# Tree attention on one core: every GpSimd store behind the last load, and V copies at later steps

## The chip, the cores and the metric

The kernel runs on one core of a Trainium2 chip. The metric is the device time of one execution in microseconds (us). A profiled execution has a span, from its first to its last instruction, and a time of its own that is a little longer than the span.

The core has a matrix engine (TensorE, PE in the profile), VectorE (DVE), ScalarE (ACT), GpSimd (POOL) and SyncE (SP). Transfers between the chip's memory and the core's are issued as instructions of GpSimd, SyncE or ScalarE and are carried out by 16 DMA engines that all of them share.

## The reference

Q, K, V and the output are float32 of shape 8 x 12 x 512 x 64 (batch, heads, positions, width): 96 heads, 12.58 MB each. A position attends to itself and to its ancestors in a binary tree laid over the positions.

```
mask[i, i] = 1
parent = i
while parent > 0:
    parent = (parent - 1) // 2
    mask[i, parent] = 1

scores = einsum('bhqd,bhkd->bhqk', Q, K) * scale
scores = scores + (1 - mask) * (-1e9)
weights = exp(scores - max(scores))
weights = weights / (sum(weights) + 1e-10)
return einsum('bhqk,bhkd->bhqd', weights, V)
```

## The kernel before

The 96 heads are worked on as 48 pairs. The outer loop has one step `i` per pair. In step `i` TensorE makes the scores of pair `i` (`scores1`, `scores2`), ScalarE takes the exponentials, TensorE multiplies the exponentials of pair `i - 1` with V (`values`, tile `ob`), and VectorE normalises pair `i - 1` (`norm`, lines 581 and 583, one reciprocal for a pair) into an output buffer `of` that holds 8 heads. There is one `ob` in the on-chip accumulation memory for all but the last pair, so the values of a pair wait until the pair before is normalised. Then the K (odd steps) or Q (even steps) of two later pairs is transposed by TensorE and copied by VectorE (`turn`: lines 401, 412, 416, 420 for K, 433 and 441 for Q). At the end of the step, VectorE does the V copies that a table gives it for this step.

K and Q come in blocks of 8 heads with four buffers each, V in blocks of 16 heads with three buffers (`vloads`). All these loads are issued by GpSimd, which turns float32 into bfloat16 on the way; V of a block comes in three pieces, "upper", "even" and "odd" rows. From heads 16 on, V is rearranged into tiles `vt` (two sets, used in turn) by copies that `spread` makes, all at line 336:

- "M" and "Y" on VectorE, 8 heads at a time, at the steps that `BY_VECTOR` and `STEADY_VECTOR` name. M needs all three pieces of the load.
- "X", "Z0", "Z1" (`spread_pool`) and four "top" copies (`spread_top`) on GpSimd. X writes over a part of what M wrote, so it comes behind M.

GpSimd works through one list in order, `pool_program`: loads, its own V copies and the stores of the output. A GpSimd instruction that waits holds everything behind it. A load waits until its buffer is free; further, GpSimd's transfers share eight completion counters in turn, so that one is issued only when the eighth before it has landed. `ready` decides only after which step an entry of the list is put into the program.

The list is written out by hand up to heads 56 to 63; from head 64 on a loop makes it. That loop issues K and Q of each block of 8, what is left of V, GpSimd's V copies, and a store of 8 heads as soon as `BEHIND` (56) heads lie between it and the load:

```
while VO * stored + VO + BEHIND <= h + KB:
    ops.append((store, nc.gpsimd, VO * stored, VO))
    stored += 1
```

With the store in the written-out part, four stores of 8 heads (1 MiB each) stand among the loads. The rest of GpSimd's stores stand behind the last load. SyncE stores heads 76 to 79 at step 41 (`store_apart`) and, with ScalarE, the last heads.

`STEADY_VECTOR` puts M of heads 64 to 79 at steps 24 and 26 and Y at 28 and 30; of heads 80 to 95, M at 32 and 34 and Y at 36 and 38.

Of the kernel before, what the change touches and what calls it, by code (L numbers as in the profile page):

```python
# [9 lines left out]

CODE = 2048.0
CODE_ROWS = 40
NOUT = 11
BEHIND = 56

# [104 lines left out]
def kernel(  # L120
# [7 lines left out]
    nc = tc.nc  # L128
# [4 lines left out]
    NH = B * H  # L133
# [3 lines left out]
    KB, VB, VO = 8, 16, 8  # L137
# [28 lines left out]
    small = ctx.enter_context(tc.tile_pool(name="small", bufs=4))  # L166
    opool = ctx.enter_context(tc.tile_pool(name="opool", bufs=NOUT))
    psS = ctx.enter_context(tc.tile_pool(name="psS", bufs=1, space=bass.MemoryType.PSUM))
# [168 lines left out]

    PARTS = ((0, 1, 2, 3, 4, 5, 6, 7, 8, 9), ("M", "X", "Y", "Z0", "Z1", 6, 7, 8, 9))

    def spread_top(o, h0=0, h1=VB):  # L340
        for part in range(6, 10):
            spread(nc.gpsimd.tensor_copy, o, part, h0, h1)

# [263 lines left out]
    def pool_program():  # L607

        ops = [
            (load_k, 2, 2), (load_q, 2, 2), (load_v, 0, 4), (load_v, 4, 4),  # L610
            (load_k, 4, 2), (load_k, 6, 2), (load_q, 4, 2), (load_k, 8, 4),
            (load_q, 6, 2), (load_q, 8, 4), (load_v, 8, 8), (load_k, 12, 4),
            (load_q, 12, 4), (load_k, 16, 4), (load_rows, 1, "upper"),
            (load_q, 16, 4), (load_rows, 1, "even"), (load_k, 20, 4), (load_rows, 1, "odd"),
            (load_q, 20, 4), (load_k, 24, 8), (load_q, 24, 4), (load_rows, 2, "upper"),
            (load_q, 28, 4), (load_k, 32, 4), (load_rows, 2, "even", "odd"),
            (load_q, 32, 8), (load_k, 36, 4), (load_rows, 3, "upper"),
            (spread_pool, (1, "Z0", 8, 16), (1, "Z1", 8, 16)),
            (load_k, 40, 8), (load_q, 40, 8), (load_rows, 3, "even", "odd"),
            (spread_top, 2, 0, 16), (spread_pool, (2, "Z0", 0, 16), (2, "Z1", 0, 16)),  # L620
            (load_q, 48, 4), (spread_pool, (2, "X", 0, 8)),
            (load_k, 48, 8), (spread_pool, (2, "X", 8, 16)),
            (load_q, 52, 4), (load_rows, 4, "upper"), (spread_top, 3, 0, 16),
            (load_k, 56, 8), (load_q, 56, 8), (load_rows, 4, "even", "odd"),
            (spread_pool, (3, "X", 0, 8), (3, "Z0", 0, 16), (3, "Z1", 0, 16), (3, "X", 8, 16)),
            (load_rows, 5, "upper"), (store, nc.gpsimd, 0, VO),
        ]
        loaded, stored = 88, 1
        for h in range(64, NH, KB):
            top = [(spread_top, h // VB + 0)] if h % VB == 8 and 4 <= h // VB + 0 < NH // VB else []  # L630
            ops += [(load_k, h, KB)] + top + [(load_q, h, KB)]
            while loaded < min(h + 32, NH):
                names = ("even", "odd") if loaded % VB else ("upper",)
                ops.append((load_rows, loaded // VB) + names)
                loaded += KB
            if top:
                o = h // VB
                ops.append((spread_pool, (o, "X", 0, 16), (o, "Z0", 0, 16), (o, "Z1", 0, 16)))
            while VO * stored + VO + BEHIND <= h + KB:
                ops.append((store, nc.gpsimd, VO * stored, VO))  # L640
                stored += 1
        for g in range(stored, NH // VO - 1):
            if g == APART // VO:
                ops.append((store, nc.gpsimd, VO * g + 2, APART - VO * g - 2))
            else:
                ops.append((store, nc.gpsimd, VO * g, VO))
        for p0, p1 in zip(SPLIT_ROWS, SPLIT_ROWS[1:]):
            ops.append((store, nc.gpsimd, APART // VO * VO, 2, 1, p0, p1))
        return ops

    def ready(op, i):
# [16 lines left out]
    BY_VECTOR = {  # L668
        0: [(0, 2, 0, 8), (0, 7, 0, 4), (0, 1, 0, 8), (0, 6, 0, 8), (0, 3, 0, 8), (0, 9, 0, 8)],
        1: [(0, 0, 4, 8)],  # L670
        2: [(0, 7, 4, 16), (0, 4, 8, 12)],
        3: [(0, 5, 8, 16), (0, 2, 8, 16), (0, 3, 8, 16)],
        4: [(0, 0, 8, 16)],
        5: [(0, 9, 12, 16)],
        6: [(0, 4, 12, 16)],
        7: [(1, "M", 0, 8), (1, "Y", 0, 8), (1, 7, 0, 8)],
# [9 lines left out]
        20: [(3, "M", 8, 16)],  # L686
        22: [(3, "Y", 0, 8)],
        24: [(3, "Y", 8, 16)],
    }
    BY_SCALAR = {  # L690
# [8 lines left out]
    }  # L699

    STEADY_VECTOR = {0: [("M", 0, 8)], 2: [("M", 8, 16)], 4: [("Y", 0, 8)], 6: [("Y", 8, 16)]}

    def spread_by(copy, table, steady, i):

        o, j = divmod(i, 8)
        todo = table.get(i, [])
        if 4 <= o + 1 < NH // VB:
            todo = todo + [(o + 1,) + piece for piece in steady.get(j, [])]
        for args in todo:
            spread(copy, *args)  # L710

    program = pool_program()
# [23 lines left out]
    for i in range(NP + 1):  # L736
        steps = FIRST[i] if i < len(FIRST) else "SVK" if i % 2 else "SVQ"
        for step in steps:
            if step == "S" and i < NP:
                scores1(i)  # L740
                scores2(i)
            if step == "V" and i >= 1:
                values(i - 1)
                norm(i - 1)
                valued = True
            if step == "K" and kdone < NP:
                kdone = turn("kst", kdone)
            if step == "Q" and qdone < NP:
                qdone = turn("qst", qdone)
            if step == "W":  # L750
                nc.scalar.copy(
                    out=codes[64:64 + CODE_ROWS, 1280:1536], in_=codes[0:CODE_ROWS, 1280:1536]
                )
            if step == "X":
                spin("s1" if valued else "ob", 2)
            if step == "D":
                spread_by(nc.vector.tensor_copy, BY_VECTOR, STEADY_VECTOR, i)
            if step == "A":
                spread_by(nc.scalar.copy, BY_SCALAR, {}, i)
        if "D" not in steps:  # L760
            spread_by(nc.vector.tensor_copy, BY_VECTOR, STEADY_VECTOR, i)
        if "A" not in steps:
            spread_by(nc.scalar.copy, BY_SCALAR, {}, i)
        pool(i)
        if i == APART_AT:
            store_apart()
        if i >= NP - 3 and i < NP:
            store(nc.sync, head(i - 1, 0), 2, 2)
# [33 lines left out]
```

## Time and profile before

| | |
|---|---|
| median of 3 runs | 135.26 us (135.2 to 137.54) |
| the profiled execution's own time | 135.11 us |
| its span | 133.2 us |
| mean granted clock of TensorE | 0.961 |
| busy: PE, DVE, ACT, POOL | 115.8, 100.0, 94.4, 77.2 us |
| read from memory, written to it | 37.94 MB, 12.58 MB |

A row of a timeline gives the start, the duration, the engine and the line, what is written and read, and in brackets how long the engine had been idle before and what ended that. L336 is line 336 of the kernel. Rows with several instructions say xN. A matmul's end is modelled, and a busy PE is not PE at its peak. The rows "DMA to landing" are from an issue to its last byte's completion. In the windows view each row is a stretch of the span, with its length, each engine's busy time, the clock granted to TensorE, the share of the DMA engines and the GB/s that were written.

### The profile page before, as it was taken

How to read it: one execution, taken by the hardware profiler on the slowest of the kernel's cores; microseconds unless marked ns; L12 is line 12 of the kernel's file. 1: busy time of each engine (PE TensorE's matmuls, PEld its weight loads, DVE VectorE, ACT ScalarE, POOL GpSimd, SP SyncE). 2: the span in 40 equal slices, each digit the busy share in tenths (PEclk: the TensorE clock that was granted, in tenths of full speed). 3: DMA queues.
4: the chain of work that ended last, by engine and by line, in shares of the span. 5: the costliest groups of instructions: out<-in, count | busy, mean ns of one | idle time of the engine just before them, and what ended most of it. 6: DMA issues, size and time to landing. Idle time of an engine off the chain costs nothing.

```text
span 133.2 us, 5532 instructions
## 1 busy us (share of the span) xinstructions
PE 115.8 (87%) x2417; PEld 80.3 (60%) x2417; DVE 100.0 (75%) x249; ACT 94.4 (71%) x153; POOL 77.2 (58%) x106
## 2 busy tenths in 40 slices
PE   6987969999898998999979399999898997989920
PEld 2543655766675766677756367677665775666610
DVE  3449779889999999969865666989797897667350
ACT  4369577988889788587858444898866887597900
POOL 6999526354285999968723789525449820005900
PEclk9999999999999999999999757999999999999995
DMA  3999999999999999999999999999999999999993
GB/s 116 233 178 191 199 196 200 202 202 205 199 202 202 202 203 205 200 210 198 206 203 198 317 253 202 292 274 252 319 216 334 231 313 401 400 393 369 379 262 132
DMA packets 32676, 32.27 MB, mean 242 GB/s; under 512 B 1628, under 2 KB 29916, under 8 KB 32652
## 3 DMA queue, kind: packets, MB, share of 16 engines
q0 software_dynamic: 30256, 29.63, 114.5%
q1 hardware_dynamic: 1836, 1.83, 4.2%
q10 hardware_dynamic: 560, 0.46, 1.1%
q8 instruction: 19, 0.31, 0.9%
q14 instruction: 5, 0.04, 0.1%
HBM read 37.94 MB, written 12.58 MB: 379 GB/s over the span
## 4 chain that ended last, share of the span: by engine, by line
PE 41%; DMA 40%; POOL 6%; issue 4%; DVE 3%; ACT 2%; DVEq 0%; ACTq 0%; POOLq 0%
DMA vst<-in_V_dram 40%; PE ob L551 13%; PE s L458 6%; PE s L466 4%; PE qtp L433 4%; PE ktp L401 4%; PE s L501 3%; PE s L491 3%; POOL kst L239 2%; POOL qst L239 2%; DVE of L583 1%; POOL vst L239 1%; PE s L551 1%; DVE vt L336 1%; ACT e L472 1%
## 5 line engine op out<-in xcount | busy, mean ns | idle before, releaser
L476 ACT ACTIVATE e<-s 128x1024 bf16<-128x1024 f32 x40 | 40.9, 1023 | 23.3 <-PE s L466 22.7
L551 PE MATMUL ob<-vt,e 128*128 128x65 bf16 (+1 forms) x940 | 38.3, 199 | 5.0 <-DVE of L583 3.5
L551 PEld LDWEIGHTS <-e 128*128 128x128 bf16 (+1 forms) x960 | 31.0, 104 | 13.4 <-DVE of L583 3.3
L507 ACT ACTIVATE e<-s 128x384 bf16<-128x384 f32 x80 | 34.7, 491 | 0.0
L583 DVE TENSOR_TENSOR of<-ob,rec 128x512 f32<-128x512 f32 x47 | 32.5, 691 | 1.6
L336 POOL COPY vt<-vst 32x512 int32<-32x512 int32 (+1 forms) x32 | 24.1, 753 | 8.8 <-DVE vt L336 4.4
L592 POOL DMA_DIRECT2D out_dram<-of x17 | 14.2, 838 | 15.6 <-DVE of L583 14.5
L336 DVE COPY vt<-vst 64x1024 bf16<-64x1024 bf16 (+6 forms) x42 | 17.9, 427 | 6.0 <-DMA vst<-in_V_dram 5.4
L458 PE MATMUL s<-codes 40*128 40x512 bf16 x96 | 19.9, 402 | 1.3 <-issue 0.7
L581 DVE RECIPROCAL rec<-ob 128x8 f32<-128x8 f32 x47 | 9.6, 205 | 14.4 <-PE ob L551 13.6
L466 PE MATMUL s<-kq 64*128 64x512 bf16 x96 | 18.9, 385 | 0.0
L280 POOL DMA_DIRECT2D vst<-in_V_dram x15 | 10.8, 720 | 13.2 <-DMA vst<-in_V_dram 7.5
L501 PEld LDWEIGHTS <-kq 64*128 64x128 bf16 x320 | 12.7, 95 | 5.5 <-issue 1.2
L501 PE MATMUL s<-kq 64*128 64x160 bf16 (+1 forms) x320 | 15.3, 210 | 0.4 <-issue 0.4
L491 PE MATMUL s<-codes 40*128 40x384 bf16 x80 | 14.1, 339 | 0.3
L401 PE MATMUL ktp<-ptile,kst 128*64 128x128 bf16 x320 | 12.9, 224 | 1.2 <-issue 0.9
L441 DVE COPY kq<-qtp 128x1024 bf16<-128x1024 bf16 x20 | 13.6, 682 | 0.4 <-PE qtp L433 0.3
L433 PE MATMUL qtp<-ptile,qst 128*64 128x128 bf16 x320 | 13.1, 224 | 0.8 <-issue 0.6
L251 POOL DMA_DIRECT2D kst<-in_K_dram x12 | 9.1, 761 | 5.7 <-DMA kst<-in_K_dram 1.5
L251 POOL DMA_DIRECT2D qst<-in_Q_dram x13 | 9.5, 728 | 4.8 <-PE s L501 1.9
L491 PEld LDWEIGHTS <-codes 40*128 40x128 bf16 x80 | 6.3, 96 | 9.3 <-issue 1.3
L472 ACT ACTIVATE e<-s 128x1024 bf16<-128x1024 f32 x8 | 8.2, 1022 | 5.0 <-PE s L466 5.0
(42 smaller groups left out, 121.6 us busy)
## 6 DMA issues: line engine op xcount, KB each, us to landing
out_dram<-of POOLq DMA_DIRECT2D x10, 1024.0 KB, 15.7
kst<-in_K_dram POOLq DMA_DIRECT2D x8, 512.0 KB, 15.2
qst<-in_Q_dram POOLq DMA_DIRECT2D x7, 512.0 KB, 16.2
vst<-in_V_dram POOLq DMA_DIRECT2D x12, 256.0 KB, 14.4
vst<-in_V_dram POOLq DMA_DIRECT2D x6, 512.0 KB, 13.6
qst<-in_Q_dram POOLq DMA_DIRECT2D x8, 256.0 KB, 11.9
kst<-in_K_dram POOLq DMA_DIRECT2D x6, 256.0 KB, 11.8
out_dram<-of SPq DMA_DIRECT2D x4, 256.0 KB, 5.4
```

The source lines that it names most:

```text
L251: return nc.gpsimd.dma_start(out=kept[b][:, h0 % KB:h0 % KB + n, :, :].rearrange("p (g x) t d -> p g (x t d)", x=2), in_=wide[:, h0 // 2:( ...
L336: return copy(out=dst, in_=src)
L401: nc.tensor.transpose(out=columns(kp[64 * a:64 * a + 64, :], mixed, (256, 2), (leaves - mixed, 2), (1, 32)), in_=st[:, 2 * i % KB // 2 + a ...
L433: nc.tensor.transpose(out=halves[64 * a:64 * a + 64, :, c:c + 64], in_=st[:, 2 * i % KB // 2 + a, 4 * u + t, :], identity=ptile[:, 0:128],)
L458: nc.tensor.matmul(out=sp[:, a, :], lhsT=(k1code if i < WIDE else k1wide)[64 * a:64 * a + CODE_ROWS, :], rhs=(q1code[64 * a:64 * a + CODE_ ...
L466: nc.tensor.matmul(out=sp[:, a, :], lhsT=keys(i, a, TOP), rhs=qTs[i][64 * a:64 * a + 64, :, :].rearrange("p t c -> p (t c)"), start=False, ...
L476: ) if i < WIDE else nc.scalar.activation(
L491: nc.tensor.matmul(out=flat[:, a, :, :].rearrange("p u (t c) -> p u t c", t=4)[:, :, :, 16:64], lhsT=k2wide[64 * a:64 * a + CODE_ROWS, :], ...
L501: nc.tensor.matmul(out=flat[:, a, :, lo:hi], lhsT=keys(i, a, WTILE2[t]), rhs=qT[64 * a:64 * a + 64, :, lo:hi], start=False, stop=t == 1, s ...
L507: nc.scalar.activation(out=e2s[i % NE][:, a, :, 32:128].rearrange("p t (r u) -> p t r u", u=2), in_=flat[:, a, :, :].rearrange("p u (t r) ...
L551: nc.tensor.matmul(out=ob[lo:hi, a, 65 * t:65 * t + 65], lhsT=e[:, a, PLACE[t], lo:hi], rhs=vt[vtile[tile_v][0]][:, head(i, a) % VB, vtile ...
L583: nc.vector.tensor_tensor(out=ofs[g][:, first:last + 1:step, :, :], in0=o4[:, a:a + n, :, 0:D], in1=rec[:, a:a + n, :, :].to_broadcast([P, ...
```

## The change

The loop from head 64 on is replaced by a list written out to its end: K and Q of heads 64 to 79, all of V's heads 80 to 95 behind the top copies of heads 64 to 79, then the rest of GpSimd's copies of that block, K and Q of heads 80 to 95, GpSimd's copies of heads 80 to 95, and after these every one of GpSimd's stores. The copies, loads and stores are the same ones as before; the four stores that stood among the loads are now behind them. The output buffers become 12 (each of 8 heads).

`STEADY_VECTOR` goes, and `BY_VECTOR` names the steps for heads 64 to 95 too: M of heads 64 to 79 at 26 and 28 (before 24 and 26), Y at 29 and 30 (before 28 and 30); M of heads 80 to 95 at 36 and 37 (before 32 and 34), Y at 38 and 39 (before 36 and 38).

```
-NOUT = 11
-BEHIND = 56
+NOUT = 12
...
-            (load_rows, 5, "upper"), (store, nc.gpsimd, 0, VO),
+            (load_k, 64, 8), (load_q, 64, 8), (load_k, 72, 8), (spread_top, 4, 0, 16),
+            (load_q, 72, 8), (load_rows, 5, "upper"), (load_rows, 5, "even", "odd"),
+            (spread_pool, (4, "X", 0, 16), (4, "Z0", 0, 16), (4, "Z1", 0, 16)),
+            (load_k, 80, 8), (load_q, 80, 8), (load_k, 88, 8), (load_q, 88, 8),
+            (spread_top, 5, 0, 16),
+            (spread_pool, (5, "X", 0, 16), (5, "Z0", 0, 16), (5, "Z1", 0, 16)),
         ]
-        loaded, stored = 88, 1
-        for h in range(64, NH, KB):
-            top = [(spread_top, h // VB + 0)] if h % VB == 8 and 4 <= h // VB + 0 < NH // VB else []
-            ops += [(load_k, h, KB)] + top + [(load_q, h, KB)]
-            while loaded < min(h + 32, NH):
-                names = ("even", "odd") if loaded % VB else ("upper",)
-                ops.append((load_rows, loaded // VB) + names)
-                loaded += KB
-            if top:
-                o = h // VB
-                ops.append((spread_pool, (o, "X", 0, 16), (o, "Z0", 0, 16), (o, "Z1", 0, 16)))
-            while VO * stored + VO + BEHIND <= h + KB:
-                ops.append((store, nc.gpsimd, VO * stored, VO))
-                stored += 1
-        for g in range(stored, NH // VO - 1):
+        for g in range(NH // VO - 1):
...
+        26: [(4, "M", 0, 8)],
+        28: [(4, "M", 8, 16)],
+        29: [(4, "Y", 0, 8)],
+        30: [(4, "Y", 8, 16)],
+        36: [(5, "M", 0, 8)],
+        37: [(5, "M", 8, 16)],
+        38: [(5, "Y", 0, 8)],
+        39: [(5, "Y", 8, 16)],
     }
...
-    STEADY_VECTOR = {0: [("M", 0, 8)], 2: [("M", 8, 16)], 4: [("Y", 0, 8)], 6: [("Y", 8, 16)]}
```

`spread_by` loses the argument for that table.

More of the change, by code (lines that the diff above doesn't have):

```diff
@@ L338, with spread_top @@
     PARTS = ((0, 1, 2, 3, 4, 5, 6, 7, 8, 9), ("M", "X", "Y", "Z0", "Z1", 6, 7, 8, 9))
-    def spread_top(o, h0=0, h1=VB):
+    def spread_top(o, h0, h1):
         for part in range(6, 10):
@@ L699, with spread_by @@
     }
-    STEADY_VECTOR = {0: [("M", 0, 8)], 2: [("M", 8, 16)], 4: [("Y", 0, 8)], 6: [("Y", 8, 16)]}
[L703 to L709, printed above, removed]
+    def spread_by(copy, table, i):
+        for args in table.get(i, []):
             spread(copy, *args)
@@ L756 @@
             if step == "D":
-                spread_by(nc.vector.tensor_copy, BY_VECTOR, STEADY_VECTOR, i)
+                spread_by(nc.vector.tensor_copy, BY_VECTOR, i)
             if step == "A":
-                spread_by(nc.scalar.copy, BY_SCALAR, {}, i)
+                spread_by(nc.scalar.copy, BY_SCALAR, i)
         if "D" not in steps:
-            spread_by(nc.vector.tensor_copy, BY_VECTOR, STEADY_VECTOR, i)
+            spread_by(nc.vector.tensor_copy, BY_VECTOR, i)
         if "A" not in steps:
-            spread_by(nc.scalar.copy, BY_SCALAR, {}, i)
+            spread_by(nc.scalar.copy, BY_SCALAR, i)
         pool(i)
```

## The prediction

> **What bounds the kernel now.** I read the page's slices first, then the windows view for the rate of the DMA in stretches of one kind, then the timelines of GpSimd and VectorE for the steps that move. The page first:
>
> ```profile
> DMA  3999999999999999999999999999999999999993
> GB/s 116 233 178 191 199 196 200 202 202 205 199 202 202 202 203 205 200 210 198 206 203 198 317 253 202 292 274 252 319 216 334 231 313 401 400 393 369 379 262 132
> HBM read 37.94 MB, written 12.58 MB: 379 GB/s over the span
> ```
>
> The DMA engines are never free between the first slice and the last. The GB/s row counts what is written: a load reads float32 and writes bfloat16, so 200 there is 400 of reading. The windows view gives both kinds (its last two columns are the DMA share and GB/s):
>
> ```profile
> core 0: us, PE busy (x) PEld busy (x) DVE busy (x) ACT busy (x) POOL busy (x), PEclk, DMA share, GB/s
> 6.00:70.00 64.00, 58.62 (x1278) 41.26 (x1274) 54.65 (x135) 50.04 (x80) 42.91 (x59) 1.00 1.35 200
> 112.00:120.00 8.00, 6.73 (x162) 4.80 (x158) 5.37 (x13) 5.92 (x12) 0.00 (x0) 1.00 1.03 398
> ```
>
> From 6 to 70 us only loads run (400 GB/s read), from 112 to 120 us only stores (398 GB/s). One common figure, 400 GB/s or 2.62 us per MiB, turns the 50.5 MB into 126.3 us of pure moving. The last store of the program and its time to landing are these:
>
> ```profile
> L592 ACTq DMA_DIRECT2D out_dram<-of x1: 351/351/351, 128.5 to 128.5; - x1
> DMA to landing us min/median/max: 3.6/3.6/3.6
> ```
>
> It lands at 128.5 + 3.6 = 132.1. So 126.3 of 132.1 us are unavoidable moving, and the rest is the start and the end. That is the first bound: **whatever order the transfers take, a stretch without any is lost**, since nothing later can go faster. The second bound is TensorE, nearly full from 84 us on. It lost time before that. VectorE's timeline (start, duration, engine, line; in brackets the idle time before it and what ended it):
>
> ```profile
> 69.79 0.21 DVE L581 RECIPROCAL rec<-ob 128x8 f32<-128x8 f32 x1 [1.28 <-PE ob L551]
> 71.35 0.42 DVE L336 COPY vt<-vst 64x1024 bf16<-64x1024 bf16 x1
> 74.16 0.43 DVE L336 COPY vt<-vst 128x1024 bf16<-128x1024 bf16 x1 [2.38 <-DMA vst<-in_V_dram]
> 83.17 0.21 DVE L581 RECIPROCAL rec<-ob 128x8 f32<-128x8 f32 x1 [0.86 <-PE ob L551]
> 85.28 0.21 DVE L581 RECIPROCAL rec<-ob 128x8 f32<-128x8 f32 x1
> 87.38 0.21 DVE L581 RECIPROCAL rec<-ob 128x8 f32<-128x8 f32 x1 [0.17 <-PE ob L551]
> 103.45 0.21 DVE L581 RECIPROCAL rec<-ob 128x8 f32<-128x8 f32 x1 [0.50 <-PE ob L551]
> ```
>
> TensorE's timeline behind that, and its clock in the windows view:
>
> ```profile
> 75.48 1.20 PE L551 MATMUL ob<-vt,e 128*128 128x65 bf16 x20 [2.28 <-DVE of L583]
> ```
>
> ```profile
> 66.50:69.80 3.30, 2.60 (x64) 1.83 (x58) 1.90 (x6) 1.88 (x5) 1.06 (x2) 1.00 1.27 203
> 76.00:80.00 4.00, 4.00 (x60) 2.75 (x59) 2.43 (x6) 1.40 (x3) 3.50 (x5) 0.50 1.16 272
> 80.00:84.00 4.00, 4.00 (x80) 2.77 (x82) 2.70 (x7) 2.18 (x5) 3.68 (x4) 0.78 1.32 201
> ```
>
> There is one L581 per pair; counted back from the last pair, 69.79 belongs to pair 23, 83.17 to pair 27 and 103.45 to pair 36. The row at 74.16 is the M copy of heads 64 to 71. VectorE waits 2.38 us in it for V, with pair 24's normalisation queued behind; TensorE has one ob buffer, so it waits 2.28 us for that normalisation, and then works at a granted clock of 0.50 and 0.78 until 84 us. An undisturbed pair takes 87.38 - 85.28 = 2.10 us.
>
> **The V copies later.** M of heads 64 to 71 goes from step 24 to step 26. Its V lands when the DMA chain says:
>
> ```profile
> 58.30 15.67 DMA vst<-in_V_dram
> ```
>
> That is 73.97. At step 26 the copy stands behind pair 25's normalisation: 69.79 + 2 x 2.10 = 73.99, and in step 24 the copy followed its pair's reciprocal by 71.35 - 69.79 = 1.56, so it starts at 75.6, 1.6 us after the landing. I cost the copies themselves at nothing, because they are the same copies. They fit beside the normalisation in a TensorE step; without that cover each costs its 0.42 us. The wait goes, and I take the clock loss with it. Pairs 23 to 27 took 83.17 - 69.79 = 13.38 us and would take 4 x 2.10 = 8.40, so **TensorE is 5.0 us earlier** from pair 27 on. Bounds: all of it, or only the wait of 2.4 us if the clock falls anyway.
>
> On that fall, the Trainium skill, TensorE: Matmul & The Clock Gate, section What's actually happening, says the half rate comes after an idle window of about 3.4 us. The trace disagrees as far as it goes: the gap was 2.28 us, and the clock was at 0.50 right behind it. By the page the gap would be too short to blame, and the fall might come again; the second rival below prices it from the rows.
>
> **The loads in a new order.** Up to the second half of V's heads 64 to 79 (the issue at 58.30) the GpSimd queue is the same. Behind it stood 10 MiB of loads mixed with four stores of 1 MiB, to this last load:
>
> ```profile
> L251 POOL DMA_DIRECT2D qst<-in_Q_dram x1: 740/740/740, 94.0 to 94.0; - x1
> DMA to landing us min/median/max: 16.2/16.2/16.2
> ```
>
> It landed at 110.2: 14 MiB in 36.2 us, 2.59 us each. Without the four stores the loads land at 73.97 + 10 x 2.59 = **99.9 us**, if GpSimd issues in time. The place to check is the load of K from head 80, now behind X, Z0 and Z1 of heads 64 to 79, and X waits for the M copy of step 28: pair 27 at 78.2, the M copy 1.56 later at 79.8, X about 0.6 after it (rows below), three copies in 3.2 us, so K 80 is issued at 83.6. The six MiB issued before it last until 73.97 + 6 x 2.59 = 89.5. The queue does not run dry, with 5.9 us in hand; the rest of the loads follow at about 0.75 us each. K, Q and V all arrive earlier than before, so TensorE gains no new wait.
>
> **The stores behind everything.** Now the first store stands behind X, Z0 and Z1 of heads 80 to 95. X may not run before the second M copy of those heads, and that copy is moved from step 34 to step 37. Step 34 of before (97.79, then GpSimd's two rows) and the K copies of step 37 (104.97) show the price of each piece:
>
> ```profile
> 97.79 0.42 DVE L336 COPY vt<-vst 128x1024 bf16<-128x1024 bf16 x1
> 104.97 0.41 DVE L420 COPY kq<-ktp 128x512 bf16<-128x512 bf16 x1
> ```
>
> ```profile
> 98.34 3.21 POOL L336 COPY vt<-vst 32x1024 int32<-32x1024 int32 x3 [3.60 <-DVE vt L336]
> 101.50 4.57 POOL L592 DMA_DIRECT2D out_dram<-of  x5
> ```
>
> Pair 36 is normalised at 103.45 - 5.0 = 98.5. The K copies of step 37 end 104.97 + 0.41 - 103.45 = 1.93 later, so M starts at 100.4, X follows M's start by 98.34 - 97.79 = 0.55, at 100.9, and the three copies take 101.50 - 98.34 = 3.16. **The first store is issued at 104.1**, where before four stores had gone out between the loads and five more followed from 101.5. In the whole of this stall GpSimd waits for VectorE and nothing else can refill the DMA queue: the last load is long issued, and the stores of SyncE come only with pair 41.
>
> So the DMA engines, which finish their last load at 99.9, have nothing until the first store's data moves. What an issue costs before data moves on empty queues is not shown for GpSimd. The nearest row is a small load at the start:
>
> ```profile
> L184 ACTq DMA_DIRECT2D ptile<-tree_eye x1: 383/383/383, 0.7 to 0.7; - x1
> DMA to landing us min/median/max: 2.6/2.6/2.6
> ```
>
> Its 64 KB take 0.2 us to move, so 2.4 us are fixed. Bounds: from 0.9 (the 4.57 / 5 of one store's issue alone) to 3.6 (the last store's landing, with other stores beside it); I take 2.4, the quietest of the three.
>
> Then all 12.58 MB of output are still to go, 31.4 us at 400 GB/s. Bounds: 31.1 at the 2.59 per MiB of the mixed stretch; 32.9 at what before's last 8 MiB took, 110.2 to 132.1 with its thin end, 2.74 per MiB. Compute is over by 128 - 5 = 123 us, so the small stores of SyncE and ScalarE at the end hide in the backlog, where before they stood open.
>
> The twelfth output buffer costs nothing: 12 buffers of 8 heads hold all 96 heads, so no normalisation waits for a store.
>
> **Sum.** 104.1 + 2.4 + 31.4 = 137.9 us for the last landing. Before, the span of 133.2 ended 1.1 after the last landing, and the profiled execution's own time, 135.11, is 1.9 over its span: 137.9 + 1.1 + 1.9 = **140.9 us**. The median of the runs is 135.26, 0.15 above the profiled one, so I forecast 141.0. In terms of the queue: it is silent for 104.1 + 2.4 - 99.9 = 6.6 us, and 0.8 of that comes back at the end.
>
> The Trainium skill, DMA: Bandwidth & Descriptors, section Anatomy of one DMA, gives about 2.0 us plus the bytes over 436 GB/s for a GpSimd DMA. No run here shows 436; the stretch of stores alone had 398. By the page the last landing would be 104.1 + 2.0 + 28.9 = 135.0 and the time an estimate of 138.0, still over before.
>
> **The rivals.**
>
> *The silent stretch is filled (not slower).* If the stores start before the loads run out, 99.9 + 31.4 = 131.3, and the time is 134.3. The place is the end of the load queue, the point from which it decides is the first issue: up to 99.9 + 0.8 - 2.4 = 98.3 nothing is lost against before. X would have to start at 95.1, 5.8 us sooner than worked out. For it: TensorE's waits on issue and code between pairs 27 and 36 are 20.28 - 9 x 2.10 = 1.4 us, which could shrink. Against: 1.4 is all there is; TensorE is at full clock and busy in that stretch. Chance 0.06.
>
> *The clock falls anyway.* TensorE gets back only the wait. Then pair 36 stands at 103.45 - 2.4 = 101.1, everything behind it moves by 2.6, and the time is 143.6. For it: the clock took until 84 us to recover, so what sets it acts over several us. Against: between 66.50 and 69.80 TensorE stood for 0.7 us (2.60 busy of 3.30) and the clock stayed at 1.00, so only a longer gap is known to lower it, and that gap goes. Chance 0.13.
>
> *Stores alone go faster than 400 GB/s.* For it: no load is beside them for 30 us, and TensorE is done for the last 14. To reach 138.0, the edge of a difference that can be told, the output would have to move in 28.5 us, at 441 GB/s; to be no slower than before in 25.7 us, at 490. Against: the pure stretch of before held 398, with TensorE idle a sixth of it. Chance 0.08.
>
> *The edit does not do what it says*, because GpSimd keeps the queue full only on paper: should X of heads 64 to 79 come over 5.9 us late, the loads run dry too. It can only add. Chance 0.03.
>
> **How the numbers follow.** The forecast has 0.70. From the bounds: 104.1 may be 102.7 (no waits on issue) to 106.7, the start 0.9 to 3.6, the drain 31.1 to 32.9, so 137.7 to 146.2 at the far ends. I cut to 138.0 to 144.5, which takes in the fallen clock and the fast stores. About 2% (2.7 us) is what a measurement of this kernel tells from no change: faster by more than that needs under 132.6, so a filled stretch and fast stores at once (0.03); within it, up to 138.0, lie the rest of the filled stretch and half of the fast stores (0.09); slower has 0.88.
>
> **What would show it.** Right: the GB/s row near 200 until 100 us, then one or two slices near empty around 100 to 106, then near 400 to the end; the first L592 of GpSimd at about 104 behind a wait on VectorE's copy; no wait on V near 74 and a full clock through 84; last reciprocals near 123, and 14 us of stores after them. Wrong: a first store before 98, a DMA row without a hole, or pair 36 much off 98.5.

## The result and the profile after

The changed kernel takes **150.76 us** (median of 4 runs, 150.49 to 151.07) against 135.26 before: 1.115 times as long, with an interval of 1.112 to 1.118. Forecast were 141.0 us, at most 144.5. The direction was right, the size was not. The profiled execution took 150.49 us, its span 147.2, with a mean granted clock of 0.932. Medians here are of all runs of a kernel, while ratios leave out the runs that fell into a slower state, so that the two need not agree to the last per cent.

The slices of the changed kernel, in the rows that answer to those of before:

```profile
PEclk9999999999999999999999999999999999755555
DMA  5999999999999999999999999990059999999960
GB/s 152 188 173 193 198 200 201 204 202 201 201 203 201 206 204 202 204 202 205 202 206 207 201 185 202 206 169 11 4 207 350 306 378 372 391 395 395 394 217 26
```

A slice is 3.7 us. The loads run at 200 written up to about 100 us, two slices are nearly empty, and then come the stores. They do not start at 400 but at 350, 306, 378, 372, and reach 391 to 395 only in the slices from about 125 us on; the last two are thin. The windows view puts lengths to this:

```profile
core 0: us, PE busy (x) PEld busy (x) DVE busy (x) ACT busy (x) POOL busy (x), PEclk, DMA share, GB/s
76.00:80.00 4.00, 4.00 (x102) 3.01 (x100) 3.51 (x10) 3.27 (x6) 0.00 (x0) 1.00 1.24 207
100.00:104.00 4.00, 4.00 (x102) 2.98 (x98) 3.31 (x10) 3.33 (x6) 0.20 (x1) 1.00 0.02 4
108.00:108.50 0.50, 0.50 (x20) 0.41 (x16) 0.49 (x2) 0.46 (x2) 0.50 (x1) 1.00 0.00 0
108.50:109.00 0.50, 0.50 (x6) 0.20 (x6) 0.43 (x3) 0.00 (x0) 0.50 (x1) 1.00 0.87 360
109.00:112.00 3.00, 2.68 (x69) 1.95 (x64) 2.60 (x6) 2.21 (x4) 3.00 (x5) 1.00 1.00 363
112.00:126.00 14.00, 10.72 (x236) 7.46 (x233) 7.12 (x17) 10.31 (x18) 5.54 (x7) 1.00 1.02 356
126.00:138.00 12.00, 1.17 (x21) 0.76 (x20) 2.02 (x6) 0.00 (x0) 2.09 (x3) 0.55 1.03 396
138.00:146.00 8.00, 0.00 (x0) 0.00 (x0) 0.00 (x0) 0.00 (x0) 1.60 (x2) 0.50 0.57 201
```

In 100 to 108.5 us the DMA engines move next to nothing (share 0.02 and 0.00); then for 14 us they are called full (share 1.02) at 356 GB/s, and for 12 us full at 396. GpSimd's timeline shows what holds the stores back:

```profile
81.57 3.20 POOL L335 COPY vt<-vst 32x1024 int32<-32x1024 int32 x3 [5.64 <-DVE vt L335]
84.72 0.77 POOL L250 DMA_DIRECT2D kst<-in_K_dram  x1
...
103.80 3.31 POOL L335 COPY vt<-vst 32x1024 int32<-32x1024 int32 x3 [12.21 <-DVE rec L580]
107.06 8.16 POOL L591 DMA_DIRECT2D out_dram<-of  x9
...
141.08 0.64 POOL L591 DMA_DIRECT2D out_dram<-of  x1 [2.04 <-DMA out_dram<-of]
```

X (line 335; the code stands one line higher than before) waits 12.21 us, and the first store is issued at 107.06. The profile puts the end of that wait to the reciprocal (`rec`) that VectorE runs right behind the M copy. X starts 0.14 us after the M copy's end (103.25 + 0.41), in the kernel before it was 0.13 (97.79 + 0.42 to 98.34), so it is the M copy that X waits for, as the kernel's order of writes demands. The last piece of the output is issued at 141.08, behind a wait for a transfer's landing. The landings of the last load, of the first store and of that last piece, from the view of single instructions:

```profile
L250 POOL DMA_DIRECT2D qst<-in_Q_dram x1: 777/777/777, 86.9 to 86.9; - x1
DMA to landing us min/median/max: 13.4/13.4/13.4
L591 POOL DMA_DIRECT2D out_dram<-of x1: 911/911/911, 107.1 to 107.1; - x1
DMA to landing us min/median/max: 4.9/4.9/4.9
L591 POOL DMA_DIRECT2D out_dram<-of x1: 637/637/637, 141.1 to 141.1; - x1
DMA to landing us min/median/max: 4.3/4.3/4.3
```

So the loads end at 86.9 + 13.4 = 100.3, data of the stores moves from about 108.55 (the engines are busy 0.87 of 108.5 to 109.0), and the output is out at 141.1 + 4.3 = 145.4: **a hole of 8.3 us and a drain of 36.9 us**, where 6.6 and 31.4 were forecast.

VectorE's timeline holds the steps towards X:

```profile
70.66 0.21 DVE L580 RECIPROCAL rec<-ob 128x8 f32<-128x8 f32 x1 [1.29 <-PE ob L550]
76.81 0.41 DVE L335 COPY vt<-vst 128x1024 bf16<-128x1024 bf16 x1
79.57 0.21 DVE L580 RECIPROCAL rec<-ob 128x8 f32<-128x8 f32 x1 [0.19 <-PE ob L550]
84.04 1.02 DVE L335 COPY vt<-vst 64x1024 bf16<-64x1024 bf16 x1
101.41 0.21 DVE L580 RECIPROCAL rec<-ob 128x8 f32<-128x8 f32 x1 [0.62 <-PE ob L550]
103.25 0.41 DVE L335 COPY vt<-vst 128x1024 bf16<-128x1024 bf16 x1
```

Pairs 23, 27 and 36 stand at 70.66, 79.57 and 101.41. The row at 76.81 is the M copy of heads 64 to 71, now without a wait. The same stretch on TensorE, and two later rows:

```profile
86.08 0.79 PE L550 MATMUL ob<-vt,e 128*128 128x65 bf16 x20 [0.54 <-DVE of L582]
93.06 0.20 PE L500 MATMUL s<-kq 64*128 64x64 bf16 x2 [0.43 <-issue]
99.25 0.47 PE L432 MATMUL qtp<-ptile,qst 128*64 128x128 bf16 x10 [0.90 <-issue]
...
117.82 0.50 PE L550 MATMUL ob<-vt,e 128*128 128x65 bf16 x11 [1.38 <-issue]
...
126.21 0.19 PE L550 MATMUL ob<-vt,e 128*64 128x65 bf16 x1 [1.87 <-issue]
```

### The profile page after: what moved, and what is told of

Read it like the earlier page. It is cut to its first block, busy times and chain, and to the rows that moved or that the text cites. A ratio compares the mean times of both kernels' runs of the same rounds, so it can differ in the third digit from the quotient of the medians.

```text
span 147.2 us, 5529 instructions
## 1 busy us (share of the span) xinstructions
PE 112.1 (76%) x2414; PEld 78.3 (53%) x2417; DVE 101.0 (69%) x249; ACT 94.5 (64%) x153; POOL 77.4 (53%) x106
## 3 DMA queue, kind: packets, MB, share of 16 engines
HBM read 37.94 MB, written 12.58 MB: 343 GB/s over the span
## 4 chain that ended last, share of the span: by engine, by line
PE 35%; DMA 23%; DVE 19%; POOL 11%; issue 5%; ACT 1%; POOLq 0%; ACTq 0%
DMA out_dram<-of 17%; PE ob L550 13%; DMA vst<-in_V_dram 7%; DVE of L582 6%; DVE vt L335 6%; PE s L457 5%; POOL out_dram L591 5%; PE ktp L400 3%; PE qtp L432 3%; PE s L465 3%; PE s L500 3%; PE s L490 3%; POOL kst L238 2%; POOL qst L238 2%; DVE rec L580 2%
## 5 line engine op out<-in xcount | busy, mean ns | idle before, releaser
L550 PE MATMUL ob<-vt,e 128*128 128x65 bf16 (+1 forms) x940 | 37.7, 197 | 7.2 <-issue 3.6
L550 PEld LDWEIGHTS <-e 128*128 128x128 bf16 (+1 forms) x960 | 30.3, 102 | 15.7 <-issue 4.2
L335 POOL COPY vt<-vst 32x512 int32<-32x512 int32 (+1 forms) x32 | 24.3, 759 | 26.1 <-DVE rec L580 12.2
L506 ACT ACTIVATE e<-s 128x384 bf16<-128x384 f32 x80 | 34.7, 490 | 0.0
L591 POOL DMA_DIRECT2D out_dram<-of x17 | 14.2, 839 | 20.5 <-DMA out_dram<-of 15.5
L335 DVE COPY vt<-vst 64x1024 bf16<-64x1024 bf16 (+6 forms) x42 | 19.1, 454 | 4.0 <-DMA vst<-in_V_dram 3.4
L580 DVE RECIPROCAL rec<-ob 128x8 f32<-128x8 f32 x47 | 9.7, 206 | 16.4 <-PE ob L550 15.8
L400 PE MATMUL ktp<-ptile,kst 128*64 128x128 bf16 x320 | 12.3, 219 | 0.3 <-DVE kq L419 0.3
L432 PEld LDWEIGHTS <-qst 128*64 128x64 bf16 x320 | 9.8, 110 | 1.7 <-issue 1.6
## 6 DMA issues: line engine op xcount, KB each, us to landing
vst<-in_V_dram POOLq DMA_DIRECT2D x6, 512.0 KB, 13.4
```

The costliest lines, as they stand in the source:

```text
L335: return copy(out=dst, in_=src)
L432: nc.tensor.transpose(out=halves[64 * a:64 * a + 64, :, c:c + 64], in_=st[:, 2 * i % KB // 2 + a, 4 * u + t, :], identity=ptile[:, 0:128],)
L506: nc.scalar.activation(out=e2s[i % NE][:, a, :, 32:128].rearrange("p t (r u) -> p t r u", u=2), in_=flat[:, a, :, :].rearrange("p u (t r) ...
L550: nc.tensor.matmul(out=ob[lo:hi, a, 65 * t:65 * t + 65], lhsT=e[:, a, PLACE[t], lo:hi], rhs=vt[vtile[tile_v][0]][:, head(i, a) % VB, vtile ...
L591: return eng.dma_start(out=Or[p0:p1, h0:h0 + step * (n - 1) + 1:step, :], in_=ofs[g][p0:p1, f:f + step * (n - 1) + 1:step, :, :].rearrange ...
```

## The experiments

Lines of the diffs are the changed kernel's unless said otherwise. Ratios are to the kernel before, run beside each experiment (medians of 135.3 to 135.84 there).

**Stores ahead of the late copies.** Four stores of 8 heads (in a second kernel two) move from behind GpSimd's last copies to just behind the last load; nothing else changes.

```
             (load_k, 80, 8), (load_q, 80, 8), (load_k, 88, 8), (load_q, 88, 8),
+            (store, nc.gpsimd, 0, VO), (store, nc.gpsimd, 8, VO),
+            (store, nc.gpsimd, 16, VO), (store, nc.gpsimd, 24, VO),
             (spread_top, 5, 0, 16),
...
-        for g in range(NH // VO - 1):
+        for g in range(4, NH // VO - 1):
```

> The changed kernel, with the first four stores of 8 heads put straight behind the last load (Q of head 88), ahead of GpSimd's copies of heads 80 to 95; the other stores stay behind those copies. Theory A (the silent stretch of the transfers, 100.3 to 108.8 us, is the main loss): the four stores are issued near 88 and keep the DMA engines moving until about 111, the rest is issued near 107 as before, so the stretch is filled and the last landing comes at about 132.7; time 136 to 138. Rival B (a long run of stores drains at the 344 GB/s that the changed kernel showed, whatever stands ahead of it): 12.58 MB from 100.3 at that rate end at 136.9, time 141 to 143. Rival C (the stores ahead hold GpSimd's copies up, and TensorE waits): pair 40 comes late and the time stays over 145.

> The same with two stores ahead. Theory A: two stores fill 5.2 us of the 8.5, a stretch of about 3.3 us stays silent; time about 145.6 if the slow drain behind it is there as in the changed kernel, about 141 if the drain goes at 400 GB/s. Rival D (the silent stretch costs more than its length, because the transfers behind a restart run slower): still a drain under 380 GB/s for 15 us after the restart.

Four ahead: 137.74 us, ratio 1.016 [1.007, 1.026], 13.0 us less than the changed kernel. GpSimd's timeline (the other stores follow from 106.28) and the windows of this run:

```profile
87.47 0.94 POOL L591 DMA_DIRECT2D out_dram<-of  x1
...
103.01 3.31 POOL L335 COPY vt<-vst 32x1024 int32<-32x1024 int32 x3 [8.84 <-DVE rec L580]
```

```profile
100.00:108.00 8.00, 7.63 (x188) 5.60 (x185) 7.17 (x18) 6.53 (x12) 4.89 (x5) 1.00 1.02 400
110.00:124.00 14.00, 12.01 (x257) 8.32 (x256) 8.44 (x19) 10.26 (x18) 5.32 (x8) 1.00 1.02 374
```

X is as late as in the changed kernel (103.01 against 103.80) and the queue still does not run dry: 400 GB/s in the stretch that was empty. So the stores' late start, and not the lateness of V in itself, carries most of the loss. What is left comes behind it: 374 GB/s from 110 to 124. The two runs with two stores ahead took 142.79 and 148.15 us; they lie between, as two stores would, but too far apart to measure anything.

**The V copies early, the rest of the change kept.** M and Y of heads 64 to 95 go back to before's steps.

```
-        26: [(4, "M", 0, 8)],  28: [(4, "M", 8, 16)],  29: Y,  30: Y,
-        36: [(5, "M", 0, 8)],  37: [(5, "M", 8, 16)],  38: Y,  39: Y,
+        24: [..., (4, "M", 0, 8)],  26: [(4, "M", 8, 16)],  28: Y,  30: Y,
+        32: [(5, "M", 0, 8)],  34: [(5, "M", 8, 16)],  36: Y,  38: Y,
```

> The changed kernel with VectorE's V copies of heads 64 to 95 at the steps of before. Theory A: M of heads 88 to 95 comes at step 34 instead of 37, three pairs of 2.1 us sooner, while the wait at 74 us and the half clock behind it come back and take some of that; first store near 102.5, silent stretch about 4 us shorter, time about 146. Rival E (the order of the loads and stores alone costs the time, the copies nothing): time stays within 1 us of 150.8.

**The two parts alone**, each as an edit of the kernel before: V late as in the changed kernel with before's list; and all of GpSimd's stores behind the last load with before's order of loads and V copies.

```
 V late alone:         + BY_VECTOR rows 26 to 39 of the change;  STEADY_VECTOR = {}
 stores behind alone:  NOUT = 12;  BEHIND = 1000;  no (store, nc.gpsimd, 0, VO);
                       loaded, stored = 88, 0
```

> The kernel before with VectorE's V copies of heads 64 to 95 at the later steps, its loads and stores unchanged. Theory A (the transfers bound the kernel): the wait at 74 us and the half clock go, TensorE is up to 5 us earlier, and the time moves by less than 1 us, 134.3 to 135.5, because the last store lands by the DMA engines' work. Rival F (TensorE bounds the second half): the time falls by 3 to 5 us to 130 to 132. Rival G: GpSimd's X copies come later, its stores and loads behind them too, and the time rises to 136 or more.

> The kernel before with nothing changed but that all of GpSimd's stores stand behind its last load and its last V copies (and 12 output buffers); loads in the order of before, V copies at the steps of before. Theory A (what counts is how long after the last load's landing the first store comes): the first store is held by X of heads 80 to 95 as in the changed kernel with the early V copies, near 100 to 102, the loads land near 100, so the time is that kernel's, 144 to 145. Rival H (the new order of the loads has a share of its own): it differs from 144.1 by more than 1 us.

| | V copies early | V copies late |
|---|---|---|
| stores among the loads | 135.26 (before) | 138.44, ratio 1.025 [1.016, 1.034] |
| stores behind, before's order of loads | 144.17, 1.061 [1.050, 1.072] | |
| stores behind, the change's order of loads | 144.09, 1.064 [1.053, 1.076] | 150.76 (the change) |

144.17 and 144.09 are the same within their intervals, about 1.5 us to either side: **the new order of the loads has no larger share in it.** (With V early, 146 had been expected and the first store near 102.5.) The two other parts cost 2.5% and 6.1% by themselves and 11.5% together, more than their sum. GpSimd's timelines say why, first with V early, then with V late among before's stores:

```profile
100.11 8.29 POOL L591 DMA_DIRECT2D out_dram<-of  x9
```

```profile
104.48 3.31 POOL L336 COPY vt<-vst 32x1024 int32<-32x1024 int32 x3 [10.96 <-DVE rec L581]
```

V early brings the first store from 107.06 to 100.11, just behind the end of the loads, and 6.7 us come off. The kernel is still 6% over before, with a hole of only some three microseconds (shares of 0.48, 0.17, 0.00 and 0.51 in the four from 98 to 102): something else than the hole is lost. V late alone holds the stores back as long as in the change, but there the load queue is longer by the four stores in it. The DMA only thins for a moment (a share of 0.86 from 108 to 110 us, of 1.04 in the two microseconds behind it), and then is slow too:

```profile
112.00:126.00 14.00, 11.88 (x227) 8.07 (x223) 7.43 (x19) 8.82 (x15) 5.54 (x8) 0.88 1.02 359
```

In the prediction V late was by itself only a gain for TensorE. Alone it costs 3.2 us, as the third of the theories above had it. By its share the thin moment loses some 0.3 us of them, and against the 389 of before in 112 to 126 us this row loses 14 x 30/400 = 1.1 us; what the rest is stays open.

**Whole stores at the end.** Heads 72 to 79 are stored by GpSimd in one piece, instead of two heads by GpSimd in six uneven pieces of rows, four by SyncE and two by themselves.

```
         for g in range(NH // VO - 1):
-            if g == APART // VO:
-                ops.append((store, nc.gpsimd, VO * g + 2, APART - VO * g - 2))
-            else:
-                ops.append((store, nc.gpsimd, VO * g, VO))
-        for p0, p1 in zip(SPLIT_ROWS, SPLIT_ROWS[1:]):
-            ops.append((store, nc.gpsimd, APART // VO * VO, 2, 1, p0, p1))
+            ops.append((store, nc.gpsimd, VO * g, VO))
...
-        if i == APART_AT:
-            store_apart()
```

> The changed kernel with heads 72 to 79 stored by GpSimd in one transfer of 128 rows, in place of SyncE's four uneven pieces, one transfer of two heads and GpSimd's six uneven pieces. Theory I (the slow drain, 344 GB/s in place of 400, comes from the uneven pieces, which load some of the 16 DMA engines more than others and go out one at a time at the end): the drain from the first store takes 32 to 33 us in place of 36.6 and the time falls to 146 to 148. Theory D (it comes from the restart after the silent stretch): the drain keeps its slow first 15 us, and the time stays at 149 to 151.

147.09 us, ratio 1.079 [1.071, 1.088]: 3.7 us less than the change by the medians, 4.8 by the ratios. In the profiled execution (148.06 us) GpSimd is done early, and the end reads

```profile
120.73 0.89 POOL L591 DMA_DIRECT2D out_dram<-of  x1 [2.61 <-DVE of L582]
138.00:146.00 8.00, 0.00 (x0) 0.00 (x0) 0.00 (x0) 0.00 (x0) 0.00 (x0) 0.50 0.61 241
```

This last store lands 23.7 us after its issue, at 144.4. Data of the stores moves from 109.98, so the drain takes 34.4 us, 2.5 less than in the change. The uneven pieces thus cost between 2.5 and 4.8 us at the end of this long drain. The same edit in the kernel before:

> The kernel before with heads 72 to 79 stored whole by GpSimd in place of the uneven pieces. If the uneven pieces cost time wherever they stand, before gets faster by 1 to 2 us, 133 to 134.5. If they balance the DMA engines in the order of before, and only the changed order makes them a burden, before gets slower or stays: 135 to 138.

135.16 us, ratio 1.0003 [0.997, 1.004]: there the pieces neither cost nor help. So this price belongs to the change, which made the piecewise end stand behind all of the output that GpSimd stores.

**The hole filled with other transfers.** Useless loads are put behind the last load and in front of the late copies: V of heads 64 to 79 (2 MiB) and K and Q of heads 64 to 71 (1 MiB each) once more, whose data nothing uses. The stores stay where the change has them.

```
             (load_k, 80, 8), (load_q, 80, 8), (load_k, 88, 8), (load_q, 88, 8),
+            (again_v,), (again, "kst", Kw), (again, "qst", Qw),
             (spread_top, 5, 0, 16),
```

The two small functions that issue these loads, and a line that admits them to the program from step 32 on, are not shown.

> The changed kernel with 4 MiB of useless loads (V of heads 64 to 79, K and Q of heads 64 to 71 once more, into buffers that nothing reads) behind the last load, so that the DMA engines stay at work until the first store. They end near 110.8, 2.0 us after the first store's data moved in the changed kernel. Theory D (a drain that follows work at once runs at about 400 GB/s; the restart is what makes it slow): the drain takes 32 to 33 us, the last landing is near 143.5, and the time 1 to 3 us under the changed kernel's although 4 MiB more are moved. Theory I or any other cause that lies in the stores themselves: the drain takes 36 us or more, and the time is 151 to 153.

148.62 us, ratio 1.095 [1.085, 1.104]: **4 MiB more are moved, and the kernel is no slower than the change**, by the medians it is 2.1 us faster. Of the 1.9 us between the two profiled executions, though, 1.3 lie outside the spans (2.0 against 3.3 us). Its last useless load and its last store:

```profile
L616 POOL DMA_DIRECT2D qst<-in_Q_dram x1: 747/747/747, 92.8 to 92.8; - x1
DMA to landing us min/median/max: 17.6/17.6/17.6
L591 POOL DMA_DIRECT2D out_dram<-of x1: 637/637/637, 140.3 to 140.3; - x1
DMA to landing us min/median/max: 4.8/4.8/4.8
```

From the last load's landing at 110.4 to 145.1 it is 34.7 us. This can't be set beside the change's 36.9 as it is, for here the first stores move beside the last loads: in the 34.7 us 345 GB/s were written, 12.0 of the output's 12.58 MB. The other 0.6 MB are another 1.5 us at 400, so the whole output takes **36.2 us, against 36.9 in the change**. Nothing was idle before it, so the drain has a loss of its own besides the hole: the time went as the theory of the restart had it, the drain as its rival. With the same loads and whole stores:

> The changed kernel with both of the two last edits: heads 72 to 79 stored whole by GpSimd, and 4 MiB of useless loads (V of heads 64 to 79, K and Q of heads 64 to 71) between the last load and the first store. If the slow drain of the changed kernel has two independent parts, the uneven pieces (36.6 to 34.4 us when they are whole) and the start on idle DMA engines (36.6 to 34.8 when they are kept busy), the drain takes 32.5 us here, near the 31.4 of 400 GB/s, and the time is 145 to 147 with loads that end near 110.5. If both edits remove the same part, the drain stays at 34 to 35 us, and the time at 147 to 149.

146.78 us, ratio 1.088 [1.080, 1.095]; the interval overlaps that of the run before. Last useless load, last store, and the rate in between:

```profile
L616 POOL DMA_DIRECT2D qst<-in_Q_dram x1: 745/745/745, 93.0 to 93.0; - x1
DMA to landing us min/median/max: 17.5/17.5/17.5
L591 POOL DMA_DIRECT2D out_dram<-of x1: 885/885/885, 120.0 to 120.0; - x1
DMA to landing us min/median/max: 23.6/23.6/23.6
```

```profile
118.00:126.00 8.00, 7.56 (x131) 5.04 (x131) 3.29 (x7) 4.86 (x8) 0.89 (x1) 0.79 1.02 379
```

From 110.5 to 143.6 it is 33.1 us at 367 GB/s, and with the 0.4 MB that moved before them the drain takes 34.2 us, 2.0 less than with uneven pieces. So nearly all that comes off is the pieces' part (34.4 without useless loads), and the filled hole adds little. The rate from 118 to 126 is 379. In these two kernels the first store is issued at 106.3 and 107.4, three to four microseconds before the last load lands. The last kernel of this row gives it more: the useless V load stands in the list twice, 6 MiB in all.

> As the kernel with whole stores and useless loads, with 2 MiB more of them (V of heads 64 to 79 twice), so that the useless loads end near 116 and the first store, issued near 108, waits about 11 us in the queue in place of 5.8. If a store that is issued onto nearly empty queues is what moves slowly (356 to 379 GB/s, where stores issued 11 to 16 us ahead moved at 389 to 401), the stretch from 118 to 126 us shows 395 GB/s or more, and the drain behind the useless loads takes 31.5 to 32.5 us. If the slowness has another cause (the steps of TensorE and VectorE beside it, or the length of the run of stores), that stretch stays at 375 to 385 and the drain at 33. Time 149 to 152 in both, as 6 useless MiB are moved.

151.31 us, ratio 1.117 [1.111, 1.124]: longer, for it moves more. What counts is its drain. The last useless load, the first store, the last store, and the same window:

```profile
L616 POOL DMA_DIRECT2D qst<-in_Q_dram x1: 747/747/747, 101.9 to 101.9; - x1
DMA to landing us min/median/max: 15.1/15.1/15.1
L591 POOL DMA_DIRECT2D out_dram<-of x1: 915/915/915, 108.7 to 108.7; - x1
DMA to landing us min/median/max: 10.9/10.9/10.9
L591 POOL DMA_DIRECT2D out_dram<-of x1: 885/885/885, 125.3 to 125.3; - x1
DMA to landing us min/median/max: 22.8/22.8/22.8
```

```profile
118.00:126.00 8.00, 6.66 (x128) 4.32 (x122) 4.95 (x12) 5.60 (x10) 3.10 (x4) 1.00 1.03 402
```

The first store is now issued 8.3 us before the last load lands (117.0), and the window shows 402 GB/s where the run before it had 379, with TensorE, VectorE and ScalarE at work in both. The work of the other engines alone can't be what slows the stores, nor can GpSimd's issuing: GpSimd was busy for 3.10 us of this window, and for 0.89 of the slower one. The number of GpSimd's transfers in flight isn't it either, for by the issues and landings it is eight at 118 us in both, and in the change too. What differs is how long the first store waited behind other transfers: it lands 10.9 us after its issue, 5.8 us in the kernel with 4 MiB, 4.9 in the change.

The drain as a whole gains little by it. From 117.0 to 148.1 it is 31.1 us, but at 369 GB/s: 1.1 MB of the output had moved before, so all of it takes 33.9 us, against 34.2. The faster start is given back at the end, which runs thin for 4 us (291, 197, 102 and 12 GB/s in the four from 144 on). Each of these drains is from one profiled execution.

**A version to keep?** Four stores ahead and M and Y of heads 80 to 95 at before's steps; then the same with whole stores.

```
+            (store, nc.gpsimd, 0, VO), ... (store, nc.gpsimd, 24, VO),      # as above
-        36: M,  37: M,  38: Y,  39: Y,
+        32: [(5, "M", 0, 8)],  34: [(5, "M", 8, 16)],  36: Y,  38: Y,
```

> The changed kernel with four stores behind the last load and ahead of GpSimd's copies of heads 80 to 95, and with VectorE's V copies of heads 80 to 95 at the steps of before (32, 34, 36, 38); those of heads 64 to 79 stay at the later steps. Theory A: no silent stretch, and the stores behind the copies are issued near 101, well ahead of need; the end is the DMA engines' work, 134 to 137. If the end is set by TensorE's end instead (near 127 in all of these kernels), it is no better than 137.7, that of four stores ahead alone.

> The changed kernel with four stores ahead of the copies of heads 80 to 95, their M and Y copies at the steps of before, and heads 72 to 79 stored whole by GpSimd. Without the uneven pieces: 134 to 135.5 if these cost time here as they do in the changed kernel; 136.2 or more if they help where the queue is never empty.

136.19 us, ratio 1.005 [1.000, 1.010], and 136.05 us, 1.0005 [0.995, 1.006]; the second lies between the two times that were expected of it and decides nothing on the pieces. In the first of them the stores behind the copies are issued from 97.9, and the windows view has

```profile
110.00:124.00 14.00, 11.69 (x225) 7.93 (x226) 7.07 (x17) 8.43 (x14) 4.15 (x6) 0.88 1.03 401
```

The full rate is back (in the second kernel it is 403). Neither is faster than the kernel before, which loses nothing to a hole either.

## Why the prediction was right in sign and wrong in size

Each step of the sum, forecast and measured in the profiled execution:

| step | forecast | measured | |
|---|---|---|---|
| K of head 80 issued | 83.6 | 84.72 | |
| last load landed | 99.9 | 100.3 | |
| pair 36 normalised | 98.5 | 101.41 | +2.9 |
| first store issued | 104.1 | 107.06 | +3.0 |
| issue to first data | 2.4 | 1.5 | -0.9 |
| drain | 31.4 | 36.9 | **+5.4** |
| last landing to the end of the span | 1.1 | 1.8 | +0.7 |
| outside the span | 1.9 | 3.3 | +1.4 |
| time | 140.9 | 150.49 | +9.6 |

**What held.** The wait for V near 74 us is gone and the clock is 1.00 from 76 to 80, where before had 0.50; the rival in which the clock falls anyway is out, although pair 36 came near the 101.1 that it gave. GpSimd kept the load queue full past X of heads 64 to 79. The loads end where they should, the hole is where it should be, and X waits for VectorE's M copy: from pair 36 to the first store it took 107.06 - 101.41 = 5.65 us, forecast were 5.6. Four stores ahead of the copies remove the hole and most of the loss.

**The step "pair 36 at 98.5"** was mis-sized: pair 36 came 2.0 us earlier than before, not 5.0. Of the 2.9 us missing, 0.87 stood at pair 23 already (70.66 against 69.79), before the moved copies begin. That is no more than executions differ: the Y copy one pair earlier starts at 66.03 in before, at 66.89 in the change, and at 65.92 to 68.39 in the runs above, none of which moves a V copy ahead of that point. Pairs 23 to 27 took 79.57 - 70.66 = 8.91 instead of 8.40. Pairs 27 to 36 took 21.84 us, not 20.28 as before. TensorE waited 0.26, 0.43 and 0.90 us on issue, where before it waited 0.38 and 0.62, and 0.54 us for a normalisation that stood behind a Y copy; that is 1.1 of the 1.6 us, and the rest is not placed. The Y copy took 1.02 us instead of 0.42, while GpSimd's three copies ran (81.57 to 84.77). The prediction had costed the moved copies at nothing, as the same copies; beside these copies of GpSimd's they are not the same, and TensorE's waits on issue, which it let vary downwards only, grew. The bound given for the first store, 106.7, was too low by 0.4.

**The step "31.4 us of drain"** failed most. The prediction took 398 GB/s from a stretch of before as the rate of all the stores from the first to the last byte, and bounded the drain at 32.9. The 36.9 us hold three losses against that.

The first is the rate. Some 360 GB/s up to 112 us and 356 up to 126 instead of 400 lose 3.5 x 40/400 + 14 x 44/400 = 1.9 us. It is low in the kernels whose first store met idle engines or waited for a few microseconds only, and near full where it was issued long before its turn:

| kernel | issue to landing of the first store behind the copies, us | GB/s, 112 to 126 us | GB/s, 118 to 126 us |
|---|---|---|---|
| the change | 4.9 | 356 | 375 |
| whole stores | 4.9 | 371 | 379 |
| stores behind alone | 5.2 | 358 | 376 |
| filled with 4 MiB, whole stores | 5.8 | 379 | 379 |
| V late alone | 6.1 | 359 | 375 |
| V early | 6.2 | 360 | 372 |
| filled with 4 MiB, uneven end | 6.6 | 370 | 391 |
| four ahead | 7.2 | 375 | 391 |
| filled with 6 MiB, whole stores | 10.9 | loads until 117 | 402 |
| before | 11.3 | 389 | 382 |
| before, whole stores | 12.2 | 400 | 399 |
| four ahead, M early, whole stores | 14.8 | 401 | 400 |
| four ahead, M early | 15.8 | 398 | 396 |

The second is the thin end, for which 31.4 has no term. In the kernel with whole stores 138 to 146 us run at 241 GB/s: 1.93 MB, 4.8 us' worth at 400, take the 6.4 us up to the last landing, a loss of 1.6. The bound of 32.9 was to take it in, but was misread. In before, 350 GB/s were written from 110.2 to 132.1, that is 7.7 MB and not the 8 MiB (8.4 MB) that the prediction counted, as the rest had moved beside the last loads. These 21.9 us thus lose 2.7 against 400, and the bound should have been 31.4 + 2.7 = 34.1, near the 33.9 to 34.4 of the kernels with whole stores.

The third is the uneven end. The prediction let the small stores of SyncE and ScalarE "hide in the backlog", and they did: ScalarE's was issued at 128.64 and landed 7.9 us later, SyncE's were issued up to 128.1 and landed within 12 us. The six pieces that GpSimd itself stores are not in the prediction. They now stand behind all of GpSimd's output, each issued 0.2 to 0.5 us after the eighth transfer before it has landed (waits of 2.0 to 3.3 us, the last issue at 141.08), and 138 to 146 us run at 201 GB/s: 1.6 MB, 4.0 us' worth, take 7.4 us, a loss of 3.4 where the whole stores lose 1.6. That makes 1.8 us for the pieces within the sum; the runs without them put it at 1.8 (medians of the two kernels with 4 MiB) to 4.8.

1.9 + 1.6 + 1.8 us, and 0.1 from 126 to 138 us, are the 5.4.

**The hole** itself came out at 8.3 us instead of 6.6: the first store was 3.0 us late, its data came 0.9 us sooner behind the issue, and the loads ended 0.4 us later.

The two small terms at the end were 2.1 us over those of before; other executions of the change have 2.1 to 3.1 us outside the span. What in the changed kernel makes them longer stays open.

The rival "stores alone go faster than 400" is refuted in the opposite direction. The Trainium skill, DMA: Bandwidth & Descriptors, section Anatomy of one DMA, with its 436 GB/s, is further off: the fastest windows of 8 us or more here show 401 to 403. For the first store of the changed kernel, which met idle engines, its estimate, 2.0 + 1.05 MB / 436 GB/s = 4.4 us, is near the 4.9 measured.

**What stays open** is what inside the DMA engines makes the stores move at 356 to 379 GB/s while the engines count as full. The wait of the first store goes with it, though not strictly (before, with 11.3 us, is at 382 from 118 to 126), and the two kernels with 4 and 6 MiB of useless loads and whole stores differ in nothing but a useless load. Eight transfers of GpSimd are in flight in the slow windows as in the fast one, so it is not simply a short queue; the trace does not tell the engines apart, so which of them waits for what isn't shown. Nor is there a run in which only the number of pieces changes that a store is cut into for the engines. Why an end of 1.5 to 2 MB runs thin, even in whole stores, isn't shown either.

## What to carry to other kernels

In a kernel that is bound by its transfers, a step that puts all stores behind something late costs more than the time in which nothing moves: here the stores behind the hole also moved below the full rate for some 18 us, and the awkward small pieces, which cost nothing among other transfers, came into the open. So price a drain by a stretch of the profile in which the queue was in the same state, not by the best rate that the trace shows, give its thin end a term, and when a stretch is taken as a measure, count the bytes that moved in it and not those that were issued for it. And keep a few large transfers, issued early, between the last load and the first thing that waits: four stores there were worth 13.0 of the 15.5 us.

## What the runs showed of the hardware that I had not expected

- Stores at a full DMA share do not always move alike: from 118 to 126 us 375 GB/s in the changed kernel, 402 in the run with 6 useless MiB, in each case with the other engines at work and eight of GpSimd's transfers in flight at 118 us.
- A Y copy of VectorE that takes 0.42 us took 1.02 us beside GpSimd's X, Z0 and Z1 copies, and the next such copy, at 105.13, took 1.07. The first ended 0.29 us after the last of GpSimd's three, and so did the same copy in two runs in which it started later and took 0.75 us (four ahead with M early, whole stores with 4 MiB): it looks as if it is held until GpSimd's copy is through. Beside GpSimd's top copies (70.41 to 73.12) one at 72.22 took 0.42.
- TensorE's waits on issue behind 105 us were 1.38 us (at 117.82) and 1.87 us (at 126.21) in the changed kernel, against 0.91 and 0.35 before. Mostly by them the 2.0 us that TensorE was ahead at pair 36 were gone at the end: VectorE's last row ends at 128.6, where 123 was forecast. Here it cost nothing, for the output was behind anyway; what lengthens these waits isn't shown.
